# Twelve of 22 feed-forward groups in seven-product form, woven by written counts, and a planner that books durations as intervals with a lag

## Chip, cores and metric

The kernel runs on one core of a Trainium2 chip. The metric is the device time of one execution in microseconds; before the change it is 2728.07 us, the median of three runs (2727.68 to 2728.62).

## What is computed

A trunk of two decoder layers over 256 tokens of width 2048 in float32: layer 0 mixes tokens with a gated DeltaNet, layer 1 with HGRN2, and each is followed by a SwiGLU feed-forward of inner width 5632. The change touches the two feed-forwards and the order of everything.

```python
def swiglu(h, w_gate, w_up, w_down):
    return (jax.nn.silu(h @ w_gate) * (h @ w_up)) @ w_down

def reference(x, ...):
    h = x
    for layer in range(DEPTH):
        ...
        h = h + gdn_mixer(...)      # layer 0; hgrn2_mixer in layer 1
        h = h + swiglu(rmsnorm(h, ffn_norm[layer]), ffn_w_gate[layer], ffn_w_up[layer], ffn_w_down[layer])
    return rmsnorm(h, final_norm)
```

## The kernel before

**Products in three parts.** Weights arrive as tiles of 128 x 1024 float32 (512 KB, `raw`, loaded by SP). ScalarE (ACT) rounds such a tile to the short format fp32r (`wh`), VectorE (DVE) subtracts to get the rest (`wl`), and TensorE (PE) forms high x high, high x low and low x high for each product. The activations stand split in the same way (`xt_h`, `xt_l`). One such weight tile with its load, its split and its products is an `Item`; `stream` takes the items in one list, prepares three ahead (`AHEAD`), and `wh` and `wl` have four buffers each, `raw` four.

**The feed-forward.** `ffn` cuts the inner width into 22 groups of 256 gate and 256 up columns. A plain group (`gate_up`) is 8 items, each 12 products of 512 columns into a two-bank PSUM tile `main`, and at its end the gate and the product with it. A seven-product group (`mixed_group`) computes the 2 x 2 blocks (two halves of the tokens, gate and up against two halves of the inner sum) with seven block products in place of eight, by Strassen's scheme in Winograd's form: 4 rounds of 4 items with 1, 2, 2 and 2 block products, each block product 2 x 3 matrix products of 256 columns into four banks `aux`. For each round two weight tiles are loaded (`sraw`), and two more tiles of sums of weight blocks are made on DVE with four additions of 512 columns; all four come from one ring of four `sraw` buffers, so that the next load of a half waits until the last addition on the tile before has read it. At its end eight DVE operations join the seven products (`p1`, `p4`, `sg`, `h1`). Sums of the activations' blocks (`mixh`, `mixl`) are made once a layer by `mix_inputs`. The finished groups are turned in pairs through DRAM (`turned`, `blocks_home`) and split again (`hth`, `htl`), and `down` multiplies them in four parts with 24, 24, 24 and 16 items; a part's result is added to the running sum in DRAM (`x_home`) by an accumulating DMA of POOL, four of 512 KB a part.

**What sets the order.** `FF_PLAN` has a line for each of the four parts: what stands alone, then the seven-product groups, the plain items among which their items are woven, and two numbers for `among`: how many plain items stand ahead of the first and behind the last woven one. `among` spreads the items evenly, in pairs. Nine groups are in seven-product form (2, 6, 7, 9, 12, 13, 15, 18, 20). PE's main products run in this list's order.

All operations of the program are recorded first (`Recorder`), then `plan` simulates the engines with booked costs (`COST`, `HOP`, `LANDING` and so on) and issues everything in the order in which it started; the order on each engine, and each queue's, is fixed by that. `price` books an operation; `late` is the time by which it should be done. For a DVE or ACT operation the booked cost is the whole time from its start to its result, and the engine is booked for as long.

Of the kernel before, what the change touches and what calls it, by code (L numbers as in the profile page):

```python
# [23 lines left out]
N_FF = 22  # L24
FF_PARTS = (6, 6, 6, 4)
FF_PLAN = (
# [4 lines left out]
)  # L31
N_HGRN = 4
LEVELS = (64, 32, 16, 8, 4, 2, 1)
# [14 lines left out]
HOP = 0.2  # L48
PE_SLACK = 1.5
TURN = 0.06  # L50
FP32_PRODUCT = 0.224
NARROW = {32: 0.027, 64: 0.063}
COST = {
    ("vector", "tensor_tensor"): (0.14, 1.065e-3),
    ("vector", "scalar_tensor_tensor"): (0.205, 1.065e-3),
    ("vector", "tensor_scalar"): (0.16, 0.7e-3),
    ("vector", "tensor_single_scalar"): (0.16, 0.7e-3),
    ("vector", "tensor_copy"): (0.15, 0.6e-3),
    ("vector", "tensor_reduce"): (0.30, 1.0e-3),
    ("vector", "tensor_tensor_scan"): (0.15, 2.1e-3),  # L60
    ("vector", "copy_predicated"): (0.20, 1.3e-3),
    ("vector", "transpose"): (0.18, 1.0e-3),
    ("vector", "reciprocal"): (0.20, 1.0e-3),
    ("scalar", "activation"): (0.235, 0.82e-3),
    ("gpsimd", "tensor_tensor"): (0.10, 2.3e-3),
    ("gpsimd", "tensor_copy"): (0.20, 0.8e-3),
    ("gpsimd", "memset"): (0.10, 0.85e-3),
    ("gpsimd", "affine_select"): (0.1, 1.05e-3),
}
MARGIN = 1.02  # L70
POW = 1.3
LANDING_OF = {"wide": 7.0, "u": 7.0}
# [13 lines left out]


class Op:
    __slots__ = ("eng", "method", "args", "kw", "cost", "lag", "main", "pred", "succ", "n", "late", "call", "tiles", "heirs", "share")

    def __init__(self, eng, method, args, kw, cost=0.0, lag=0.0, main=False):
        self.eng, self.method, self.args, self.kw = eng, method, args, kw
        self.cost, self.lag, self.main = cost, lag, main
# [63 lines left out]
class Recorder:  # L157
# [110 lines left out]
    def price(self, op, out):  # L268
        n = int(np.prod(out.shape[1:]))
        if op.method == "dma_start":  # L270
            op.cost, op.lag = ISSUE[op.eng], LANDING[op.eng]
            op.share = n * out.shape[0] / (P * 1024)
            if (v := self.virtual(out)) and v.tag in LANDING_OF:
                op.lag = LANDING_OF[v.tag]
        elif op.eng == "tensor":
            if op.method == "matmul" and op.args[1].dtype == F32R:
                op.cost = 0.0133 + n / 2400.0
            elif op.method == "transpose":
                op.cost = 0.112
            else:  # L280
                m = op.args[1].shape[1]
                op.cost = NARROW[m] if m <= 64 else max(FP32_PRODUCT, n * 1.69e-3)
        else:
            fixed, each = COST[op.eng, op.method]
            if op.method == "tensor_reduce":
                n = int(np.prod(op.kw["in_"].shape[1:]))
            op.cost = (fixed + each * n) * MARGIN
            if op.kw.get("accum_out") is not None:
                op.cost += ACCUMULATE
            if op.eng == "gpsimd" and op.kw.get("op") == ALU.pow:  # L290
                op.cost = POW
# [24 lines left out]
    def plan(self):  # L316
# [6 lines left out]
        t = 0.0  # L323
# [4 lines left out]
        end = t  # L328
        for op in reversed(ops):
            late = min((s.late for s in op.succ + op.heirs if s.n > op.n), default=end)  # L330
            late -= op.cost + op.lag + HOP
# [55 lines left out]
        while len(order) < len(ops):  # L387
            e, at = min(
                ((e, s) for e in clock if (s := start_of(e)) is not None), key=lambda x: x[1]
            )  # L390
            while waiting[e] and waiting[e][0][0] <= at:
                _, n, op = heapq.heappop(waiting[e])
                heapq.heappush(ready[e], (op.late, n, op))
            op = heapq.heappop(ready[e])[2] if ready[e] else mains.pop()
            wait = place(op, at)
            if wait is not None:
                if isinstance(wait, tuple):
                    starved.setdefault(wait, []).append(op)
# [12 lines left out]
            self.at[op.n] = at  # L411
            order.append(op)
            done = at + op.cost
            clock[e] = at + max(0.45, LOAD_EVERY * op.share) if e == "sync" else done
            for v in op.tiles:
                v.left -= 1
                v.free = max(v.free, done + op.lag + HOP)
                if not v.left:
                    v.pool.slots[v.tag].append((v.free, v.slot))
                    for other in starved.pop((v.pool, v.tag), ()):  # L420
                        ready_at[other.n] = max(ready_at[other.n], at)
                        release(other)
            for s in op.succ:
                if e == "none" or s.eng == "none":
                    t = at
                elif e == "sync" and s.eng == e:
                    t = done
                elif s.eng == e and (e == "tensor" or not s.pred[op]):
                    t = done + op.lag
# [81 lines left out]
    return [c[:, at : at + 1024] for c in chunks for at in range(0, c.shape[1], 1024)]  # L511


def among(few, many, head, tail):

    out, done = [], 0
    for i, item in enumerate(many):
        out.append(item)
        upto = max(0, min(len(few), -(-len(few) * (i + 1 - head) // (len(many) - head - tail))))
        upto = upto // 2 * 2  # L520
        out += few[done:upto]
        done = upto
    return out


class Trunk:
# [359 lines left out]
    def ffn(self, j, after):  # L886
        nc, a = self.nc, self.a
        hts, h1s, quick, done = {}, {}, {}, set()
# [197 lines left out]
        items, waiting = [], None  # L1086
        for part, steps in enumerate(FF_PLAN):
            for step in steps.split(" | "):
                few, _, rest = step.partition(" : ")
                if not rest:  # L1090
                    items += gate_up(int(step))
                    continue
                beside, tail = rest.split(" : ")
# [6 lines left out]
                spare = (int(n) for n in tail.split())  # L1100
                items += among([i for g in few.split() for i in mixed_group(int(g))], many, *spare)
# [925 lines left out]
```

## Time and profile before

| | us |
|---|---|
| median of three runs | 2728.07 |
| the profiled execution | 2730.16 |
| its span, first to last instruction | 2728.5 |
| of it DeltaNet stage, first feed-forward, HGRN2 stage, second feed-forward | about 817, 695, 496, 720 |
| DVE busy in these four stretches | 624.85, 568.18, 365.67, 578.76 |
| ACT busy in them | 518.43, 389.21, 293.46, 394.90 |
| DMA: moved over the span | 599.64 MB, 220 GB/s in the mean |

A line of a group reads: source line, engine, operation, output<-inputs, shapes, count, then busy us and mean ns of one, then the engine's idle time before it with who ended it. All operations have one line number, that of `issue`, since they are recorded first, so groups are told apart by the names of their tiles. A row of waits reads: who waited <- for whom: total us, times, longest. A row of the timeline or of the chain starts with its time from the span's start and its length. A row of stretches has, after the stretch and its length, busy us and count for PE, PE's weight loads, DVE, ACT and POOL, then the clock granted to PE, the share of the DMA engines and GB/s. PE's rows overlap each other, so that the distance of starts, not the length of a row, is what a product costs.

### The profile page before, as it was taken

The numbers are of one execution on the slowest core, as the hardware profiler recorded it, in microseconds if no ns is written. First come the engines' busy times: TensorE is split into PE (matmuls) and PEld (weight loads), VectorE is DVE, ScalarE is ACT, GpSimd is POOL, SyncE is SP. The second block draws the span as 40 slices with busy tenths as digits, with TensorE's granted clock in tenths as the row PEclk, the third lists the DMA queues.
The fourth block names the chain that finished last, engine by engine and source line by source line (L and its number), as shares of the span: only waits on it lengthen the run. The fifth ranks groups of instructions, "written<-read, shape, count | busy, mean of one in ns | idle before, by whom it ended". The sixth has DMA issues, their size and how long they took to land.

```text
span 2728.5 us, 44570 instructions
## 1 busy us (share of the span) xinstructions
PE 2707.1 (99%) x16966; PEld 2352.0 (86%) x16966; DVE 2137.5 (78%) x3221; ACT 1596.0 (58%) x2246; POOL 326.6 (12%) x466
## 2 busy tenths in 40 slices
PE   9999999999999999999999999999999999999998
PEld 9888888888888888888888989988888888888886
DVE  7787888777758788888788688788578788888786
ACT  6646667566565555565555656556465555555554
POOL 2213222232110000000100100000110000000010
PEclk9999999999999999999999999999999999999999
DMA  8686578687686677777776755555776777677775
GB/s 277 202 282 213 188 224 242 212 262 209 214 241 211 219 232 217 238 219 223 243 229 213 238 168 185 166 167 178 198 262 206 229 217 237 223 225 226 232 230 194
DMA packets 173959, 599.64 MB, mean 220 GB/s; under 512 B 21674, under 2 KB 22842, under 8 KB 173616
## 3 DMA queue, kind: packets, MB, share of 16 engines
q1 hardware_dynamic: 138912, 503.15, 56.2%
q0 software_dynamic: 34544, 92.79, 13.6%
q8 instruction: 133, 2.18, 0.3%
q10 hardware_dynamic: 288, 0.85, 0.1%
q14 instruction: 82, 0.67, 0.1%
HBM read 550.52 MB, written 48.28 MB: 219 GB/s over the span
## 4 chain that ended last, share of the span: by engine, by line
PE 94%; DVE 2%; DMA 2%; ACT 1%; issue 1%; SPq 0%; POOLq 0%; POOL 0%; ACTq 0%; DVEq 0%
PE main L498 77%; PE aux L498 18%; DMA sraw<-in_ffn_gu 1%; DVE wl L498 1%; DVE turned L498 0%; DMA raw<-in_ffn_gu 0%; ACT wh L498 0%; DVE sraw L498 0%; DMA first<-in_x 0%; ACT dec L498 0%; DVE htl L498 0%; DVE h L498 0%; DVE utmp L498 0%; DVE pre L498 0%; SPq L498 0%
## 5 line engine op out<-in xcount | busy, mean ns | idle before, releaser
L498 ACT ACTIVATE wh<-raw 128x1024 fp32r<-128x1024 f32 x801 | 846.6, 1060 | 846.9 <-PE main L498 732.2
L498 DVE TENSOR_TENSOR wl<-raw,wh 128x1024 fp32r<-128x1024 f32 x801 | 980.9, 1227 | 404.8 <-ACT wh L498 389.2
L498 PE MATMUL main<-wh,xt_h 128*128 128x512 f32 x1600 | 626.1, 391 | 0.8 <-ACT wh L498 0.8
L498 PE MATMUL main<-wl,xt_h 128*128 128x512 f32 x1600 | 625.6, 391 | 1.3 <-DVE wl L498 1.3
L498 PE MATMUL main<-wh,xt_l 128*128 128x512 f32 x1600 | 625.2, 391 | 0.0
L498 ACT ACTIVATE wh<-sraw 128x1024 fp32r<-128x1024 f32 (+1 forms) x288 | 272.1, 950 | 170.2 <-PE main L498 100.5
L498 DVE TENSOR_TENSOR wl<-sraw,wh 128x1024 fp32r<-128x1024 f32 (+1 forms) x288 | 307.5, 1087 | 71.1 <-ACT wh L498 70.6
L498 PEld LDWEIGHTS main<-wh,xt_l 128*128 128x128 f32 x1600 | 300.4, 188 | 62.4
L498 PEld LDWEIGHTS main<-wh,xt_h 128*128 128x128 f32 x1600 | 300.3, 188 | 61.4 <-ACT wh L498 1.2
L498 PEld LDWEIGHTS main<-wl,xt_h 128*128 128x128 f32 x1600 | 300.4, 188 | 60.6 <-DVE wl L498 1.6
L498 PE MATMUL main<-xt_h,wh 128*128 128x256 f32 (+1 forms) x1040 | 288.7, 278 | 0.7 <-ACT wh L498 0.7
L498 PE MATMUL main<-xt_h,wl 128*128 128x256 f32 (+1 forms) x1040 | 288.3, 277 | 0.9 <-DVE wl L498 0.9
L498 PE MATMUL main<-xt_l,wh 128*128 128x256 f32 (+1 forms) x1040 | 288.1, 277 | 0.3 <-DVE xt_l L498 0.3
L498 PE MATMUL main<-wh,hth 128*128 128x512 f32 x688 | 268.8, 391 | 0.9 <-ACT hth L498 0.9
L498 PE MATMUL main<-wl,hth 128*128 128x512 f32 x688 | 269.0, 391 | 0.1
L498 PE MATMUL main<-wh,htl 128*128 128x512 f32 x688 | 268.0, 390 | 0.2
L498 PE MATMUL aux<-wl,mixh 128*128 128x256 f32 x864 | 239.6, 277 | 3.2 <-DVE wl L498 3.2
L498 PE MATMUL aux<-wh,mixh 128*128 128x256 f32 x864 | 239.2, 277 | 0.1
L498 PE MATMUL aux<-wh,mixl 128*128 128x256 f32 x864 | 239.1, 277 | 0.0
L498 PEld LDWEIGHTS main<-xt_h,wh 128*128 128x128 f32 (+1 forms) x1040 | 194.4, 187 | 1.3 <-ACT wh L498 0.9
L498 PEld LDWEIGHTS main<-xt_h,wl 128*128 128x128 f32 (+1 forms) x1040 | 194.4, 187 | 1.2 <-DVE wl L498 1.1
L498 PEld LDWEIGHTS main<-xt_l,wh 128*128 128x128 f32 (+1 forms) x1040 | 194.4, 187 | 1.0 <-DVE xt_l L498 0.5
(241 smaller groups left out, 3948.0 us busy)
## 6 DMA issues: line engine op xcount, KB each, us to landing
raw<-in_ffn_gu SPq DMA_DIRECT2D x208, 512.0 KB, 4.7
raw<-in_ffn_d SPq DMA_DIRECT2D x176, 512.0 KB, 5.0
sraw<-in_ffn_gu SPq DMA_DIRECT2D x144, 512.0 KB, 5.9
raw<-in_hgrn_in SPq DMA_DIRECT2D x128, 512.0 KB, 4.1
raw<-in_gdn_kq SPq DMA_DIRECT2D x64, 512.0 KB, 5.5
raw<-in_gdn_v SPq DMA_DIRECT2D x64, 512.0 KB, 4.6
raw<-in_gdn_z SPq DMA_DIRECT2D x64, 512.0 KB, 4.9
raw<-in_gdn_out SPq DMA_DIRECT2D x64, 512.0 KB, 5.3
```

Source lines behind the costliest of these rows:

```text
L498: getattr(getattr(tc.nc, op.eng), op.method)(*args, **kw)
```

## The change

```diff
@@ -24,10 +24,10 @@
 FF_PLAN = (
-    "0 | 2 : 1 3 4 5 : 6 2",
-    "6 7 9 : 8 down 10 11 : 4 4",
...
+    "0 | 2 4 : 1 3 5 : 010000413403001303131130",
+    "6 7 9 11 : 8 down 10 : 0041413002012050340022061033120300062102",
+    "12 13 15 17 : 14 down 16 : 0111053032003031304050231322022202002501",
...
@@ -49,24 +49,26 @@
+PRODUCT = 0.1136
...
 COST = {
-    ("vector", "tensor_tensor"): (0.14, 1.065e-3),
...
+    ("vector", "tensor_tensor"): (0.065, 1.055e-3),
...
-    ("scalar", "activation"): (0.235, 0.82e-3),
+    ("scalar", "activation"): (0.14, 0.82e-3),
...
+TAIL = {"vector": 0.08, "scalar": 0.095}
@@ -274,7 +276,7 @@
             if op.method == "matmul" and op.args[1].dtype == F32R:
-                op.cost = 0.0133 + n / 2400.0
+                op.cost = PRODUCT * n / 256
@@ -285,6 +287,7 @@
             op.cost = (fixed + each * n) * MARGIN
+            op.tail = TAIL.get(op.eng, 0.0)
@@ -428,9 +431,9 @@
                 elif s.eng == e and (e == "tensor" or not s.pred[op]):
                     t = done + op.lag
                 elif s.eng == "tensor" and not s.main:
-                    t = done + op.lag + HOP + PE_SLACK
+                    t = done + op.lag + op.tail + HOP + PE_SLACK
                 else:
-                    t = done + op.lag + HOP
+                    t = done + op.lag + op.tail + HOP
@@ -511,15 +514,11 @@
-def among(few, many, head, tail):
+def woven(few, many, pattern):
-    out, done = [], 0
-    for i, item in enumerate(many):
-        out.append(item)
-        upto = max(0, min(len(few), -(-len(few) * (i + 1 - head) // (len(many) - head - tail))))
-        upto = upto // 2 * 2
-        out += few[done:upto]
-        done = upto
+    out, few = [], iter(few)
+    for item, n in zip(many, pattern):
+        out += [item] + [next(few) for _ in range(int(n))]
     return out
```

Groups 4, 11 and 17 change from the plain to the seven-product form in each layer, so that twelve of 22 have it. The even spreading gives way to a written digit for each plain item: so many seven-product items follow it. The fourth line keeps its groups and gets digits too. In the planner the fixed part of every DVE and ACT cost is cut by about what its rows overlap the next one, and that much is added as a lag (`tail`) ahead of whoever needs the result; a fp32r product of 256 columns is booked at 0.1136 in place of 0.12. `tail` is taken off in `late` and added where a tile comes free, too.

By count of instructions PE loses 576 products of 512 columns and gains 1008 of 256; DVE gets 96 additions of 512 columns more, 24 more short and 72 more long splits of `sraw` tiles, 48 fewer of `raw` tiles, and the six groups' ends; ACT the same splits; SP issues 48 `sraw` loads in place of 48 `raw` ones. Everything else keeps its number.

Two places in the order matter below. The first is DVE, in the second stretch of the first feed-forward, from the addition that frees a ring buffer to the first additions on the tile loaded into it. Before, from the group's joint (freed by the first row, read anew in the last; `x2` is two in a row):

```order
L498 TENSOR_TENSOR sraw_1775_11244<-sraw_1775_11244,sraw_1757_11095 128x512
L498 TENSOR_TENSOR sraw_1793_11291<-sraw_1781_11212 128x512
L498 TENSOR_TENSOR h1_1645_10698<-h1_1645_10698,sg_1747_11205 128x256
L498 TENSOR_TENSOR h1_1645_10698<-h1_1645_10698,sg_1748_11281 128x256
L498 TENSOR_TENSOR wl_1777_11308<-sraw_1775_11244,wh_1776_11294 128x1024
L498 TENSOR_TENSOR wl_1780_11315<-raw_1778_11164,wh_1779_11305 128x1024
L498 TENSOR_TENSOR wl_1783_11331<-sraw_1781_11212,wh_1782_11320 128x2x256
L498 STREAM_TRANSPOSE turned_1749_11342<-h1_1645_10698 128x256 x2
L498 TENSOR_TENSOR sraw_1793_11291<-sraw_1784_11296,sraw_1781_11212 128x512
```

With the change, at one of its joints (the last row reads the new tile `sraw_1891`):

```order
L501 TENSOR_TENSOR sraw_1885_11805<-sraw_1885_11805,sraw_1879_11709 128x512
L501 STREAM_TRANSPOSE turned_1838_11827<-h1_1631_10594 128x256 x2
L501 TENSOR_TENSOR wl_1884_11836<-sraw_1882_11704,wh_1883_11820 128x1024
L501 STREAM_TRANSPOSE turned_1838_11827<-h1_1631_10594 128x256
L501 TENSOR_TENSOR sraw_1894_11848<-sraw_1888_11784 128x512
L501 STREAM_TRANSPOSE turned_1838_11827<-h1_1631_10594 128x256
L501 TENSOR_TENSOR wl_1887_11856<-sraw_1885_11805,wh_1886_11842 128x1024
L501 TENSOR_TENSOR sraw_1894_11848<-sraw_1891_11830,sraw_1888_11784 128x512
```

Between the two ends stood two long splits, a short one, one addition and four smaller operations; now there stand two long splits, one addition and four transposes.

The second place is ACT in the DeltaNet stage, the third block of 24 decay rows (`dec` from `g_row`) of a head group among the weight splits `wh`. Before:

```order
L498 ACTIVATE wh_4431<-raw_4285 128x1024
L498 ACTIVATE junk_66,so_4462<-aux_4452 128x128 x4
L498 ACTIVATE dec_4484<-g_row_3569,shift_360 128x64 x24
L498 ACT_TABLE_LOAD
L498 ACTIVATE dec_4484<-dec_4484 128x1536
```

With the change:

```order
L501 ACTIVATE wh_4181<-raw_4076 128x1024
L501 ACTIVATE junk_66,so_4206<-aux_4198 128x128 x4
L501 ACTIVATE dec_4226<-g_row_3296,shift_346 128x64 x5
L501 ACTIVATE wh_4238<-raw_4107 128x1024
L501 ACTIVATE dec_4226<-g_row_3296,shift_346 128x64 x9
L501 ACTIVATE wh_4269<-raw_4140 128x1024
L501 ACTIVATE dec_4226<-g_row_3296,shift_346 128x64 x9
L501 ACTIVATE wh_4302<-raw_4171 128x1024
L501 ACTIVATE dec_4226<-g_row_3296,shift_346 128x64
L501 ACT_TABLE_LOAD
```

Three weight splits, which stood behind the block, now stand in it; the two blocks of 24 ahead of this one stay whole, and elsewhere runs of six rows between splits have become runs of nine.

More of the change, by code (lines that the diff above doesn't have):

```diff
@@ L51 @@
 FP32_PRODUCT = 0.224
+PRODUCT = 0.1136
 NARROW = {32: 0.027, 64: 0.063}
 COST = {
-    ("vector", "tensor_tensor"): (0.14, 1.065e-3),
[L55 to L61, printed above, removed]
+    ("vector", "tensor_tensor"): (0.065, 1.055e-3),
+    ("vector", "scalar_tensor_tensor"): (0.127, 1.06e-3),
+    ("vector", "tensor_scalar"): (0.08, 0.7e-3),
+    ("vector", "tensor_single_scalar"): (0.08, 0.7e-3),
+    ("vector", "tensor_copy"): (0.07, 0.6e-3),
+    ("vector", "tensor_reduce"): (0.22, 1.0e-3),
+    ("vector", "tensor_tensor_scan"): (0.07, 2.1e-3),
+    ("vector", "copy_predicated"): (0.16, 1.3e-3),
     ("vector", "transpose"): (0.18, 1.0e-3),
-    ("vector", "reciprocal"): (0.20, 1.0e-3),
-    ("scalar", "activation"): (0.235, 0.82e-3),
+    ("vector", "reciprocal"): (0.12, 1.0e-3),
+    ("scalar", "activation"): (0.14, 0.82e-3),
     ("gpsimd", "tensor_tensor"): (0.10, 2.3e-3),
@@ L88 @@
 class Op:
-    __slots__ = ("eng", "method", "args", "kw", "cost", "lag", "main", "pred", "succ", "n", "late", "call", "tiles", "heirs", "share")
+    __slots__ = ("eng", "method", "args", "kw", "cost", "lag", "main", "pred", "succ", "n", "late", "tail", "call", "tiles", "heirs", "share")
     def __init__(self, eng, method, args, kw, cost=0.0, lag=0.0, main=False):
         self.eng, self.method, self.args, self.kw = eng, method, args, kw
-        self.cost, self.lag, self.main = cost, lag, main
+        self.cost, self.lag, self.main, self.tail = cost, lag, main, 0.0
         self.pred, self.succ = {}, []
@@ L330, in plan @@
             late = min((s.late for s in op.succ + op.heirs if s.n > op.n), default=end)
-            late -= op.cost + op.lag + HOP
+            late -= op.cost + op.lag + op.tail + HOP
             op.late = min(op.late, late) if op.main else late
@@ L416, in plan @@
                 v.left -= 1
-                v.free = max(v.free, done + op.lag + HOP)
+                v.free = max(v.free, done + op.lag + op.tail + HOP)
                 if not v.left:
@@ L1092, in ffn @@
                     continue
-                beside, tail = rest.split(" : ")
+                beside, pattern = rest.split(" : ")
                 many = []
@@ L1099, in ffn @@
                         many += gate_up(int(g))
-                spare = (int(n) for n in tail.split())
-                items += among([i for g in few.split() for i in mixed_group(int(g))], many, *spare)
+                few = [i for g in few.split() for i in mixed_group(int(g))]
+                assert len(pattern) == len(many) and sum(map(int, pattern)) == len(few)
+                items += woven(few, many, pattern)
             assert waiting is None
```

3 rows, old and new, of the table FF_PLAN are left out of this document.

## The prediction

> **What bounds the kernel now.** I read the page first, then who waits on PE, then the chain of waits for PE's pace, then the stretches of the feed-forward stages.
>
> ```profile
> span 2728.5 us, 44570 instructions
> PE 2707.1 (99%) x16966; PEld 2352.0 (86%) x16966; DVE 2137.5 (78%) x3221; ACT 1596.0 (58%) x2246; POOL 326.6 (12%) x466
> ...
> PE aux L498 <- DVE wl L498: 3.2, 4, 0.9
> PE main L498 <- DVE wl L498: 2.2, 2, 1.3
> PE main L498 <- ACT wh L498: 1.5, 2, 0.8
> ```
>
> PE is busy 99% and waits for others only some 7 us in these three rows, with no wait over 1.3 us. So the time is the number of PE's products times their pace, and a change gains by taking products away and loses by making PE wait. The pace:
>
> ```profile
> 946.50 21.79 PE main L498 x96
> ...
> 901.22 0.28 PE L498 MATMUL aux<-wh,mixh 128*128 128x256 f32 x1
> ...
> 903.84 0.28 PE L498 MATMUL aux<-wh,mixl 128*128 128x256 f32 x1
> ```
>
> The first row is 96 products of 512 columns in a row: 21.79/96 = 0.2270 us each. The other two are the first and the last of 24 products of 256 columns: (903.84 - 901.22)/23 = 0.1139 us each, half of it, though a row lasts 0.28 us, since products overlap.
>
> The engine to watch behind PE is DVE. In the second stretch of a feed-forward stage, where three seven-product groups are woven into plain ones:
>
> ```profile
> 970.00:1130.00 160.00, 159.00 (x928) 140.06 (x927) 132.42 (x157) 91.92 (x102) 10.16 (x14) 1.00 0.77 229
> ...
> 1084.83 8.44 DMA sraw<-in_ffn_gu
> 1275.33 8.02 DMA sraw<-in_ffn_gu
> 2275.55 7.86 DMA sraw<-in_ffn_gu
> 2465.45 7.92 DMA sraw<-in_ffn_gu
> ```
>
> DVE (third number with a count) is busy 132.42 of 160 us, ACT 91.92, PE 159.00, at a granted clock of 1.00. The four later rows are the only ring loads on the chain that ended last: one in the second and one in the third stretch of each layer. Each is followed by one of the four waits "PE aux <- DVE wl" above.
>
> **The change part by part.** *Products.* Six groups (three a layer) change form. Each loses 96 products of 512 columns, 96 x 0.2270 = 21.79 us, and gains 4 x 2 x 7 x 3 = 168 of 256 columns, 168 x 0.1139 = 19.14 us. The gain is 2.65 us a group, **-15.9 us** in all. All of it lies on the path, since PE is the bound.
>
> The Trainium skill ("TensorE: Matmul & The Clock Gate", Back-to-back issue gap) has a warm product cost its columns over 2.4 GHz and a fixed 2.5 ns, which speaks against many short products. By that the two forms would be 20.7 and 18.3 us, and the gain an estimated 14.2 us, 1.7 less than the sum takes. The rows above show no such fixed part here (0.2270 against 2 x 0.1139).
>
> *DVE.* What such a group asks of it, beside a plain one:
>
> ```profile
> L498 DVE TENSOR_TENSOR wl<-raw,wh 128x1024 fp32r<-128x1024 f32 x801 | 980.9, 1227 | 404.8 <-ACT wh L498 389.2 <-PE aux L498 3.6 <-PE main L498 2.0
> L498 DVE TENSOR_TENSOR sraw<-sraw,sraw 128x512 f32<-128x512 f32 x216 | 146.9, 686 | 18.6 <-DMA sraw<-in_ffn_gu 17.8
> L498 DVE SCALAR_TENSOR_TENSOR p<-aux,rstd,p 128x256 f32<-128x256 f32 x36 | 17.3, 481 | 0.6
> L498 DVE TENSOR_TENSOR p<-aux,p 128x256 f32<-128x256 f32 x36 | 15.2, 422 | 1.9 <-PE aux L498 0.9
> L498 DVE TENSOR_TENSOR h<-h,sg 128x256 f32<-128x256 f32 x36 | 14.5, 418 | 0.0
> L498 DVE TENSOR_TENSOR h<-aux,sg 128x512 f32<-128x512 f32 x18 | 12.3, 681 | 0.0
> ...
> 1084.11 0.68 DVE L498 TENSOR_TENSOR sraw<-sraw,sraw 128x512 f32<-128x512 f32 x1
> 1084.71 0.69 DVE L498 TENSOR_TENSOR sraw<-sraw 128x512 f32<-128x512 f32 x1
> 1085.32 0.75 DVE L498 TENSOR_TENSOR h<-h,sg 128x256 f32<-128x256 f32 x2
> 1086.01 1.23 DVE L498 TENSOR_TENSOR wl<-sraw,wh 128x1024 fp32r<-128x1024 f32 x1
> 1087.15 1.22 DVE L498 TENSOR_TENSOR wl<-raw,wh 128x1024 fp32r<-128x1024 f32 x1
> 1088.95 0.69 DVE L498 TENSOR_TENSOR wl<-sraw,wh 128x512 fp32r<-128x512 f32 x1 [0.59 <-ACT wh L498]
> 1089.56 0.76 DVE L498 STREAM_TRANSPOSE turned<-h 128x256 f32<-128x256 f32 x2
> 1093.29 1.29 DVE L498 TENSOR_TENSOR sraw<-sraw,sraw 128x512 f32<-128x512 f32 x2 [2.97 <-DMA sraw<-in_ffn_gu]
> ```
>
> Starts stand closer than durations: an add of 512 starts 0.60 us before the next (1084.11, 1084.71), a split of 1024 1.14 us (1086.01, 1087.15); some 0.08 us overlap. By these starts a seven-product group has 16 adds (9.6), 4 short splits (2.4), 12 long ones (13.7), eight operations at its end (by the four rows about 3.7 less 8 x 0.08: 3.1) and its share of turning, about 1.2: 30.0 us. A plain one has 8 long splits (9.1), two products with the gate (0.8) and the turning: 11.1. So DVE has 18.9 us more to do a group. The second stretch of a layer then has 4 x 30.0 + 2 x 11.1 + 24 x 1.14 = 169.6 us of DVE work beside 4 x 19.14 + 2 x 21.79 + 288 x 0.2270 = 185.5 us of PE: 91%, where it was 80% (151 of 188). The third is alike, the first has about 90%, the last is unchanged in its sum. DVE does not become the bound, but its free time in a full stretch falls from 37 to 16 us, so a delay is made good more slowly. At the joint of two groups PE's first product into a bank also stands right behind the read of that bank (groups 12 and 13). I take one wait a layer at the longest that PE shows above, 1.3 us, less a little: **+2**. Bounds: 0, and one such wait at each of the eight joints a layer, +21.
>
> *The ring of loads.* This is the term that decides. A seven-product group reads 8 loads of 512 KB through a ring of four tiles, and the next load of a half waits until the last add on the old one is done. What DVE has in its order between that add and the first add on the new tile covers the load. Counted in the built order with the starts above, the cover was never under 4.8 us: 4 of 144 loads had 4.8, 22 had 5.1. Now 20 of 192 loads have 4.8 or less (3.5 to 4.7), and 16 more up to 5.15. The four at 4.8 before are the four chain rows. The DVE rows just shown are the first of them: the add at 1084.11 frees the tile, DVE runs out of work at 1090.32, the load lands at 1084.83 + 8.44 = 1093.27, and PE feels it:
>
> ```profile
> 1083.96 1.19 POOL L498 DMA_DIRECT2D x_home<-x  x1 [23.76 <-ACT sg L498]
> ...
> 1094.11 0.28 PE L498 MATMUL aux<-wh,xt_l 128*128 128x256 f32 x1
> 1094.49 0.38 PE L498 MATMUL aux<-wh,mixh 128*128 128x256 f32 x1
> 1095.78 0.39 PE L498 MATMUL aux<-wl,mixh 128*128 128x256 f32 x1 [0.91 <-DVE wl L498]
> ...
> sraw<-in_ffn_gu SPq DMA_DIRECT2D x144, 512.0 KB, 5.9
> x_home<-x POOLq DMA_DIRECT2D x52, 512.0 KB, 8.6
> ```
>
> Two starts are late by 0.26 and 1.17 us beside the pace, 1.4; with the smaller three I price a late load at 1.1 us, so 4.4 us are paid now. The load is slow (8.44 against a median of 5.9) because POOL had just issued an accumulation into x_home, which takes 8.6. How many of the 20 meet one? Four transfers fall in a stretch of 185 us; each disturbs loads issued over about 8.6 + 5.9 us, 58 of 185, so 6 of 20 if they fell at random, and all 20 if they are as aligned as the four were. I take 9, nearer to chance, since the new digits spread the loads: 9 x 1.1 - 4.4 = **+5.5**. Bounds: -4.4 (none) and (20 + 16/2) x 1.1 - 4.4 = +26.4.
>
> *The planner's costs.* All stages are put in a new order. In the feed-forward and HGRN2 stages little can move, PE waiting there only for the rows named. In the DeltaNet stage the waits "PE main" above (2.2 and 1.5) follow blocks of 24 decay rows on ACT that no weight split interrupts:
>
> ```profile
> 294.04 5.86 ACT dec L498 x24
> ...
> L498 ACT ACTIVATE wh<-raw 128x1024 fp32r<-128x1024 f32 x801 | 846.6, 1060 | 846.9 <-PE main L498 732.2
> ```
>
> Three such blocks stood there; two remain, and the third is cut into runs of 5, 9, 9 and 1 with a split between. That saves about half of those waits. Against it, runs of 6 became runs of 9 elsewhere: 5.86/24 = 0.244 us a row, so 9 rows and a split of 1.06 take 3.3 us where a weight item lasts 12 x 0.2270 = 2.72, half a microsecond late a run, over some ten such runs; the three items split ahead should hide it. I take **-1**. Bounds: -3.7 (all these waits gone) and +5.
>
> Loads of plain weights, stores and the kernel's end keep their number. The sum: -15.9 + 2 + 5.5 - 1 = **-9.4**. The profiled execution took 2730.16 us around its span of 2728.5, the median of three runs is 2728.07; applied to the median the forecast is **2719 us**.
>
> **Rivals.** *(a) The ring is no tighter in practice: 2711.* Only as many loads are late as before, so -15.9 - 1. For it: half of the loads land within the median of 5.9 us, and DVE's own idle time adds to the cover. Against: DVE has less idle time now.
>
> *(b) The ring decides, slower: 2740.* All 20 loads up to 4.8 us and half of the next 16 come late: +26.4 - 15.9 + 2 = +12.5. It overtakes the gain from (15.9 + 4.4)/1.1 = about 18 late loads on. For it: before, four of four at the edge were late. Against: these four were one place repeated four times.
>
> *(c) DVE is the bound: 2740.* If an operation kept DVE for its whole duration (0.08 us more than the starts say), a seven-product group would take 33.6 us, a plain one 12.2, and the second stretch 4 x 33.6 + 2 x 12.2 + 24 x 1.23 = 188 us against 185.5 of PE: +2.5 in each of four such stretches, and with no free time left each of the 20 loads would cost its 1.1 (+17.6 over now): +10 + 17.6 - 15.9 = +12. Against it stand the starts 0.60 us apart. The Trainium skill ("VectorE: DVE Perf Modes", Terms, DRAIN) says that the next operation cannot issue until the pipe is empty, which read as the whole duration would make this the outcome; the trace does not bear that reading out (0.60 between starts, 0.68 long).
>
> *(d) The new order costs in DeltaNet: 2726.* The runs of nine come late after all: +5 and some of the saved wait back. For it: three items of lead hid runs of six, and no run of nine but one stands in the trace. Against: that one brought no wait on PE.
>
> **How the numbers follow.** Forecast 0.48, (a) 0.22, (b) 0.13, (c) 0.04, (d) 0.13. The likeliest one's own range is 2714 to 2725. To hold 8 in 10 the range takes in (a) and (d) and stops short of (b): 2709 to 2734. A change under 0.2% (5.5 us, 2722.6 to 2733.5) cannot be told from none. Faster: 0.40 of the forecast, all of (a), 0.04 of (d): 0.66. Slower: 0.09 of (b) and (c): 0.13. Same: 0.21.
>
> **What would show it.** In the new profile, 3456 "aux<-...mixh/mixl" products at starts of 0.114 us confirm the first term. DVE should read 90 to 96% in the second stretch (83% in the row above). "PE aux <- DVE wl" should be about ten waits and some 10 us; four waits speak for (a), twenty or more for (b), and "DVE wl <- ACT wh" near nothing for (c). "PE main <- ACT wh" or "<- DVE wl" over 5 us before 817 us speaks for (d). The forecast is wrong if PE's waits together exceed some 20 us, or if the time falls under 2709.

## The result, and the profile after

The changed kernel takes **2735.22 us** (median; 2728.51 to 2741.69) against 2727.68 us before (2726.27 to 2730.79): ratio 1.0029, 95% interval 1.0023 to 1.0035. It is 0.29% slower, where 2719 us was forecast. The profiled execution took 2737.94 us.

The page of the changed kernel: its first rows, the chain that ended last by engine, one row of its groups and one of its transfers:

```profile
span 2736.2 us, 45703 instructions
PE 2704.2 (99%) x17398; PEld 2367.1 (87%) x17398; DVE 2235.8 (82%) x3401; ACT 1631.4 (60%) x2300; POOL 326.1 (12%) x466
...
PE 85%; DVE 6%; DMA 6%; ACT 1%; issue 1%; POOL 0%; SPq 0%; POOLq 0%; DVEq 0%; ACTq 0%
...
L501 DVE TENSOR_TENSOR sraw<-sraw,sraw 128x512 f32<-128x512 f32 x288 | 194.2, 687 | 37.1 <-DMA sraw<-in_ffn_gu 36.5
...
sraw<-in_ffn_gu SPq DMA_DIRECT2D x192, 512.0 KB, 5.1
```

In the kernel before the chain's row was:

```profile
PE 94%; DVE 2%; DMA 2%; ACT 1%; issue 1%; SPq 0%; POOLq 0%; POOL 0%; ACTq 0%; DVEq 0%
```

PE is still busy 99%, and with fewer columns to multiply. But the chain now lies 6% on DMA and 6% on DVE, where it was 2% and 2%, and the additions of the ring waited 36.5 us for their loads instead of 17.8. The loads' median is lower than before (5.1 against 5.9), so it is not the typical load that is late. Who waits, in the changed kernel (us in total, times, longest):

```profile
PE main L501 <- DVE wl L501: 6.5, 8, 0.9
PE aux L501 <- DVE wl L501: 4.7, 7, 1.6
PE aux L501 <- DMA first<-in_x: 2.2, 1, 2.2
PE aux L501 <- ACT wh L501: 1.6, 1, 1.6
...
DVE sraw L501 <- DMA sraw<-in_ffn_gu: 48.6, 36, 3.5
...
ACT wh L501 <- DMA sraw<-in_ffn_gu: 55.6, 31, 5.2
```

In the kernel before, DVE's row was 11 waits and ACT's 4:

```profile
DVE sraw L498 <- DMA sraw<-in_ffn_gu: 17.8, 11, 3.0
...
ACT wh L498 <- DMA sraw<-in_ffn_gu: 16.3, 4, 4.5
```

PE's own rows look harmless: they list a delay only where it is long. The better measure is PE's starts. For each product of 512 or 256 columns I took the time to the next start and subtracted 0.2272 or 0.1136 us, which is what the new planner books for it. Summed over the two feed-forward stages (812 to 1515 us, and from 2010 us on), PE started late by 12.2 us before and by 31.6 us in the changed kernel. The experiments below use this sum as "PE late".

One late load of the changed kernel, as the timeline shows it (start, us, engine, line, operation, tiles; in brackets the idle time before and who ended it):

```profile
2170.08 0.56 POOL L501 DMA_DIRECT2D blocks_home<-turned  x1 [35.38 <-DVE turned L501]
2170.80 0.70 DVE L501 TENSOR_TENSOR sraw<-sraw,sraw 128x512 f32<-128x512 f32 x1
2171.34 0.69 SPq L501 DMA_DIRECT2D sraw<-in_ffn_gu  x1
...
2173.84 0.56 POOL L501 DMA_DIRECT2D turned<-blocks_home  x1 [3.20 <-ACT wh L501]
2175.04 1.64 POOL L501 DMA_DIRECT2D turned<-blocks_home  x3 [0.64 <-issue]
...
2179.83 0.69 DVE L501 TENSOR_TENSOR sraw<-sraw 128x512 f32<-128x512 f32 x1 [3.48 <-DMA sraw<-in_ffn_gu]
2179.84 0.28 PE L501 MATMUL aux<-wh,mixh 128*128 128x256 f32 x1
...
2181.71 0.39 PE L501 MATMUL aux<-wl,mixh 128*128 128x256 f32 x1 [1.60 <-DVE wl L501]
```

The addition at 2170.80 frees the tile and SP issues the next load at 2171.34. POOL's transfers for turning h run beside it, and it lands only about 8.4 us later. DVE has nothing else to do for 3.48 us, then catches up, and PE's product at 2181.71 starts 1.87 us after the one before instead of 0.11. No accumulation into x_home is near. The prediction had named only those as what slows a load.

Counted over the 192 ring loads of this trace: 84 had no transfer of POOL on either DRAM tile beside them (median 4.6 us, 5 of them over 6.5), 51 ran beside one on x_home (median 6.4, 25 over 6.5) and 57 beside the turning alone (median 6.3, 25 over 6.5). Of the 36 additions that waited for a load, 14 (17.2 us of the 48.6) waited for one that had run beside a transfer on x_home, 21 (30.4 us) for one beside the turning alone, and one (1.0 us) for one beside neither. In the kernel before it was the other way round: 8 of the 11 waits (14.9 of 17.8 us) were for loads beside a transfer on x_home.

### The profile page after: what moved, and what is told of

Read it like the earlier page. It is cut to its first block, busy times and chain, and to the rows that moved or that the text cites. A ratio compares the mean times of both kernels' runs of the same rounds, so it can differ in the third digit from the quotient of the medians.

```text
span 2736.2 us, 45703 instructions
## 1 busy us (share of the span) xinstructions
PE 2704.2 (99%) x17398; PEld 2367.1 (87%) x17398; DVE 2235.8 (82%) x3401; ACT 1631.4 (60%) x2300; POOL 326.1 (12%) x466
## 4 chain that ended last, share of the span: by engine, by line
PE 85%; DVE 6%; DMA 6%; ACT 1%; issue 1%; POOL 0%; SPq 0%; POOLq 0%; DVEq 0%; ACTq 0%
PE main L501 67%; PE aux L501 18%; DMA sraw<-in_ffn_gu 4%; DVE wl L501 3%; DVE sraw L501 1%; ACT wh L501 1%; DVE turned L501 1%; ACT dec L501 0%; DMA raw<-in_gdn_kq 0%; DMA raw<-in_ffn_gu 0%; DMA turned<-blocks_home 0%; DVE h L501 0%; DMA blocks_home<-turned 0%; DVE p L501 0%; DVE htl L501 0%
## 5 line engine op out<-in xcount | busy, mean ns | idle before, releaser
L501 PE MATMUL main<-wh,xt_h 128*128 128x512 f32 x1408 | 551.4, 392 | 1.2 <-ACT wh L501 1.2
L501 PE MATMUL main<-wh,xt_l 128*128 128x512 f32 x1408 | 551.2, 391 | 0.0
L501 ACT ACTIVATE wh<-sraw 128x1024 fp32r<-128x1024 f32 (+1 forms) x384 | 362.8, 952 | 310.5 <-PE main L501 176.4
L501 DVE TENSOR_TENSOR wl<-sraw,wh 128x1024 fp32r<-128x1024 f32 (+1 forms) x384 | 412.7, 1087 | 45.5 <-ACT wh L501 44.1
L501 PE MATMUL aux<-wl,mixh 128*128 128x256 f32 x1152 | 321.4, 279 | 5.0 <-DVE wl L501 4.7
L501 PE MATMUL aux<-wh,mixh 128*128 128x256 f32 x1152 | 319.7, 278 | 1.6 <-ACT wh L501 1.6
L501 PE MATMUL aux<-wh,mixl 128*128 128x256 f32 x1152 | 319.7, 278 | 0.0
L501 PEld LDWEIGHTS aux<-wl,mixh 128*128 128x128 f32 x1152 | 217.0, 188 | 12.0 <-DVE wl L501 7.8
L501 DVE TENSOR_TENSOR sraw<-sraw,sraw 128x512 f32<-128x512 f32 x288 | 194.2, 687 | 37.1 <-DMA sraw<-in_ffn_gu 36.5
L501 PEld LDWEIGHTS aux<-wh,mixh 128*128 128x128 f32 x1152 | 217.3, 189 | 6.0 <-ACT wh L501 1.8
```

Of the source, the lines that this page charges most:

```text
L501: getattr(getattr(tc.nc, op.eng), op.method)(*args, **kw)
```

## The experiments

All runs in one table. "PE late" is the sum defined above; the last column is the row "DVE sraw <- DMA sraw" (us and times). Ratios are against runs of the kernel before on the same chip. Its medians there were 2727.68 to 2729.12 us, so a difference between the medians of two rows is uncertain by up to some 1.4 us.

| run | median us | ratio to before (95%) | PE late, us | DVE waits for ring loads |
|---|---|---|---|---|
| before | 2727.68 | 1 | 12.2 | 17.8, 11 |
| changed | 2735.22 | 1.0029 (1.0023 to 1.0035) | 31.6 | 48.6, 36 |
| old_costs | 2790.6 | 1.0229 (1.0215 to 1.0243) | 83.1 | 55.7, 38 |
| new_costs | 2727.28 | 0.9994 (0.9986 to 1.0003) | 7.3 | 4.5, 7 |
| no_ring_loads | 2713.53 | 0.9948 (0.9936 to 0.9961) | 11.5 | none |
| ring5 | 2723.18 | 0.9977 (0.9968 to 0.9986) | 17.4 | 18.7, 17 |
| no_x_home | 2725.62 | 0.9990 (0.9981 to 0.9999) | 23.4 | 36.7, 25 |
| no_turn | 2730.47 | 1.0006 (0.9997 to 1.0015) | 25.8 | 21.9, 16 |
| no_side | 2722.79 | 0.9979 (0.9969 to 0.9988) | 18.7 | 12.7, 10 |
| before_no_ring | 2724.95 | 0.9985 (0.9976 to 0.9994) | 7.0 | none |
| inplace | 2739.2 | 1.0040 (1.0027 to 1.0052) | 35.2 | none |
| before_inplace | 2733.77 | 1.0017 (1.0008 to 1.0026) | 15.0 | none |
| s0_ring5 | 2729.57 | 1.0004 (0.9995 to 1.0013) | 27.6 | none |
| even | 2745.06 | 1.0063 (1.0050 to 1.0076) | 47.1 | 31.2, 28 |
| land8_ring5 | 2715.25 | 0.9952 (0.9938 to 0.9965) | 11.4 | 1.3, 1 |
| land8_ring4 | 2843.08 | 1.0426 (1.0412 to 1.0440) | 146.5 | 15.0, 10 |
| land8_six | 2727.34 | 0.9994 (0.9986 to 1.0003) | 7.4 | 0.3, 1 |

### Which part of the change costs

**old_costs.** The changed kernel with the planner's table of before.

```diff
-    ("vector", "tensor_tensor"): (0.065, 1.055e-3),
+    ("vector", "tensor_tensor"): (0.14, 1.065e-3),
...
-TAIL = {"vector": 0.08, "scalar": 0.095}
+TAIL = {}
...
-                op.cost = PRODUCT * n / 256
+                op.cost = 0.0133 + n / 2400.0
```

> The changed kernel with the planner's costs of before (twelve groups, the new digits). Three theories for the 17 us between the forecast of the sum of products (2712) and the 2735 measured. T1, late ring loads: the cover of the ring is about as thin here (22 of 192 loads at 4.8 us or less, 20 in the changed kernel), so 2731 to 2737. T2, VectorE is nearly full and makes delays good too slowly: its work is the same, so 2733 to 2737. T3, the new order (its waits and the clock drops behind them): all of it goes, 2720 to 2727.

(2735 less 2712 is 23 us; the 17 there is a slip.) It came out at 2790.6, far outside all three. The written digits only work together with the new costs. With the old ones the order makes PE wait for h itself as well:

```profile
PE aux L501 <- DVE wl L501: 17.9, 21, 2.0
PE main L501 <- DVE htl L501: 9.8, 6, 2.4
PE main L501 <- ACT hth L501: 9.7, 5, 2.4
```

In the changed kernel's list the second of these rows is missing and the third is one wait of 0.3 us. So T3 in the form "the new costs are what is paid for" falls; the costs are needed.

**new_costs.** The kernel before with the new table alone (the reverse of that diff, applied to the kernel before).

> The kernel before (six groups, even weaving) with the new planner's costs alone. T1: 6 of 144 loads at 4.8 us or less against 4, so 2727 to 2731. T2: 2726 to 2730. T3, the new order: 2734 to 2740, with the clock at half at some 220 and 490 us as in the changed kernel.

2727.28 us, no change that can be told, within the ranges of T1 and T2. T3 falls here too. Under the unchanged total two things moved: DVE's waits for ring loads fell from 17.8 to 4.5 us and PE late from 12.2 to 7.3; what took that gain away again is in the table of stages further down.

**no_ring_loads.** The two halves of a weight piece (the tiles that one round of a seven-product group loads) come from two tiles loaded once a layer.

```diff
-                    item(kk, halves[0], keep(0), [(1, lambda k: k * 512)], lambda x: quarters(x)[:, 0]),
+                    item(kk, None, keep(0), [(1, lambda k: k * 512)], lambda x: quarters(x)[:, 0], kept(0, halves[0])),
...
-                return self.tile(self.pool, [P, 1024], "sraw", bufs=4, ordered=True)
+                return self.tile(self.pool, [P, 1024], "sraw", bufs=2, ordered=True)
```

> The changed kernel with the ring's loads left out: each layer loads two halves of a weight group once and all seven-product groups read these two tiles, so the groups' values are not the reference's; additions, splits and products stay in number. T1: no wait for a ring load is left, so 2719 to 2724. T2: VectorE has the same work, so 2731 to 2736. T3: 2731 to 2736.

2713.53 us, 21.7 less than the changed kernel, below even T1's range. So more than the whole loss hangs on the ring's loads. By itself this run can't tell their lateness from their traffic, which is gone with them; ring5 and land8_ring5 below keep every load. The run also decides T2 as it was put. In the second stretch (us, then busy time and count of PE, PEld, DVE, ACT, POOL, granted clock, DMA share, GB/s), first the changed kernel:

```profile
970.00:1130.00 160.00, 158.77 (x977) 141.50 (x976) 145.27 (x185) 94.43 (x105) 13.21 (x19) 1.00 0.77 232
```

and without the ring's loads:

```profile
970.00:1130.00 160.00, 160.00 (x1001) 143.93 (x1000) 148.68 (x186) 97.63 (x108) 13.21 (x19) 1.00 0.51 143
```

DVE is even fuller here, 148.68 of 160 us or 93%, and PE is never idle. A DVE at 93% does not by itself hold PE up. Whether a DVE with more free time would pass on less of a late load was not tried.

**ring5.** Five ring tiles; room comes from a scratch tile in bfloat16 and from the last rows' tile lying in h1.

```diff
-                return self.tile(self.pool, [P, 1024], "sraw", bufs=4, ordered=True)
+                return self.tile(self.pool, [P, 1024], "sraw", bufs=5, ordered=True)
...
-        self.junk = t([P, 512], "junk")
+        self.junk = t([P, 512], "junk", mybir.dt.bfloat16)
```

> The changed kernel with a ring of five tiles instead of four (room for it from a 2-byte scratch output of squares and from the last rows' tile lying in h1): 8 of 192 loads have a cover of 4.8 us or less instead of 20, the median cover is 8.1 us instead of 6.4. T1: 2720 to 2727. T2: 2732 to 2736. T3: 2732 to 2736.

2723.18 us, T1's case: 12 of the 21.7 us are back with every load, addition and product still there, and the traffic no smaller.

### What makes the loads late

**no_x_home** leaves out the accumulations of the first three parts; **no_turn** leaves out the turning's way through DRAM; **no_side** leaves out both.

```diff
             self.nc.scalar.activation(more, ps, AF.Copy)
-            self.nc.gpsimd.dma_start(self.x_cols(self.x_home, cg), more, accum_op=ALU.add)
```

```diff
-        self.nc.gpsimd.dma_start(home, blocks)
...
-        return out
+        return blocks
```

> The changed kernel with the 24 accumulations of the first three parts into x_home left out (their sums are missing in the output). After the first four runs the ring's loads carry the loss; open is what makes them late. A, the accumulations alone, as the prediction had it: most of the 21.7 us that leaving out the ring's loads gave, so 2715 to 2720. B, the transfers that turn h through DRAM as well: VectorE stood 17.2 us before late ring loads that met an accumulation and 30.4 us before such that met a turning, so a third of 21.7, 2726 to 2730. C, the thin cover with no collision: 2733 to 2736.

> The changed kernel with the way through DRAM left out of the turning (five transfers of POOL a pair of groups; the pairs' values stay unturned, so the output is not the reference's). A: 2733 to 2736. B: two thirds of 21.7 gone, 2719 to 2724. C: 2733 to 2736.

> The changed kernel without the accumulations of the first three parts into x_home and without the way of the turning through DRAM (both left out, so the output is not the reference's). One by one they gave 9.6 and 4.7 us of the 21.7 that the ring's loads cost. If collisions are all of it: 2713 to 2717. If the two only add up and the rest is the thin cover beside the other weight loads: 2719 to 2723.

The accumulations are worth 9.6 us (2735.2 less 2725.6), the turning 4.7, both 12.4, as in the second case of no_side. Neither A nor B was right in size: the accumulations weigh more than B's share and the turning less, and A's "most of 21.7" is not reached either. With both gone, 9 us of the 21.7 remain, so loads are late also without a collision with POOL's transfers. The trace of no_side shows beside what: 141 of its ring loads shared over 3 us with other weight loads and nothing of POOL's (median 4.9 us, longest 7.8), 45 shared less (median 3.9, longest 4.9). That the other weight loads are the reason was not tried by a run.

**before_no_ring.** The kernel before, its ring's loads left out in the same way as in no_ring_loads.

> The kernel before with its ring's loads left out in the same way (two halves a layer are loaded once; the groups' values are not the reference's). The prediction priced what late ring loads cost there at 4.4 us: 2723 to 2725. If its eleven waits of VectorE for a ring load cost 1.1 us each: 2714 to 2718. If nothing of them reaches TensorE: 2727 to 2729.

2724.95 us: late ring loads cost the kernel before 4.1 us (against 2729.06 in the same set of runs), and 4.4 was the prediction's price.

### More cover: three ways

**inplace** and **before_inplace** write the four sums over the loaded tiles, so that a piece takes two ring tiles instead of four. **s0_ring5** does so for the first two sums only, with five tiles.

```diff
-                        raws[2] = t[:, 0]
-                        add(t[:, 0], b11, b12)
-                        add(t[:, 1], b22, b12)
+                        add(b11, b11, b12)
+                        add(b12, b22, b12)
...
-                        add(t[:, 0], b22, raws[2])
-                        add(t[:, 1], t[:, 0], b21)
+                        add(b22, b22, b11)
+                        add(b21, b22, b21)
```

> The changed kernel with the four sums of a weight piece written over the two loaded tiles instead of into two more tiles of the ring, so that four tiles hold two pieces instead of one; all transfers, additions, splits and products stay. Counted in the built order the cover of a ring load rises from a median of 6.4 to 13.6 us, none under 6. If the wait for the ring loads is what costs: 2712 to 2717, as without these loads. If it was their traffic that slowed other things: 2723 to 2735. If additions in place wait for ScalarE's split of the same tile: 2718 to 2725 with 'DVE sraw <- ACT wh' in the waits.

> The kernel before with the same sums in place. The prediction priced its late ring loads at 4.4 us (four of them): 2722 to 2725. If only few of VectorE's 17.8 us of waits for them reach TensorE: 2726 to 2728. If eleven late loads cost 1.1 us each: 2714 to 2718.

> The changed kernel with five ring tiles and only the first pair of sums of a weight piece written over its loaded tile, so that a piece takes three tiles instead of four; counted in the built order the cover is never under 6 us (median 14.9). If late loads are the whole loss and the first sums can wait for the short split of 512 columns: 2713 to 2718. If sums in place cost as much as in the run with all four in place: 2728 to 2740.

inplace and before_inplace missed all their cases, with 2739.2 and 2733.8 us; s0_ring5, with 2729.6, is in its second. Almost no load is late any more. In the run inplace, and then in the changed kernel, ACT waits for DVE's sums:

```profile
ACT wh L501 <- DVE sraw L501: 84.4, 63, 3.4
...
PE aux L501 <- DVE wl L501: 12.4, 12, 2.0
```

```profile
ACT wh L501 <- DVE sraw L501: 25.2, 23, 3.1
```

A sum in place must wait until both splits of the loaded tile have read it, and the next split must wait for the sum. The late loads were exchanged for a longer chain of dependence between ACT and DVE; in s0_ring5 the row reads 96.1 us. These runs therefore say nothing on the price of the loads.

**even.** Twelve groups with the kernel before's spreading by pairs.

```diff
-    "0 | 2 4 : 1 3 5 : 010000413403001303131130",
+    "0 | 2 4 : 1 3 5 : 4 2",
```

> The changed kernel with its twelve groups spread evenly in pairs, as the kernel before spreads its six, instead of by the written digits; 16 of 192 loads have a cover of 4.8 us or less and 52 of 5.15 or less, against 20 and 36. If the cover at the edge decides: 2732 to 2742. If the digits bring the late loads by their bursts of four or more items: 2720 to 2728. If VectorE needs the digits to keep up: over 2745.

2745.06 us, 3 us beyond the first case and just inside the third (over 2745). The digits are worth 10 us over even pairs. The ring does not explain it: DVE waits less for ring loads here than in the changed kernel (31.2 us against 48.6), yet PE late is 47.1 us against 31.6, and PE waits for the splits:

```profile
PE aux L501 <- DVE wl L501: 20.5, 24, 1.6
```

In the changed kernel that row is 4.7 us in 7 waits. So the digits may bring late loads, and still pay by keeping the splits in time, which is the third case; no run tells this from other reasons.

### What the planner believes of a load

The planner takes 4.8 us for a load to land. With that figure it needs no more than 4.8 us of cover. **land8_ring5** and **land8_ring4** are ring5 and the changed kernel with 8.0 us; **land8_six** is new_costs with 8.0 us.

```diff
-LANDING_OF = {"wide": 7.0, "u": 7.0}
+LANDING_OF = {"wide": 7.0, "u": 7.0, "sraw": 8.0}
```

> The changed kernel with five ring tiles, and the planner told that a ring load lands after 8.0 us instead of 4.8; no sums in place. Counted in the built order 2 of 192 loads have a cover under 6 us (14 under 5.5 and 28 under 6 with five tiles alone, 52 and 74 in the changed kernel), with a median of 9.8. If the planned cover is what makes loads late: 2713 to 2718. If the later order takes VectorE's place from the plain splits: 2723 to 2732.

> The changed kernel with four ring tiles and the planner's landing time of a ring load at 8.0 us alone. 16 of 192 loads keep a cover of 4.8 us or less (20 before), 32 are under 5.5 (52 before). By the number of thin covers: 2728 to 2733. If the planner's figure alone were the fault: 2715 to 2724.

> The kernel before (six groups, even weaving, four ring tiles) with the new planner's costs and the landing time of 8.0 us: no cover under 5.0 us. Leaving out its ring's loads gave 4.1 us: if the cover is the cause, 2723 to 2727; if the loads' waits there are of another kind, 2727 to 2730.

land8_ring5 takes **2715.25 us**, 0.48% faster than the kernel before and 0.73% faster than the changed kernel. This is its first case. It is the fastest kernel that computes the reference. The collisions are still there (53 of its 192 ring loads run beside a transfer on x_home and 58 beside the turning, 51 and 57 in the changed kernel), and its loads are no faster. PE's and DVE's waits in it:

```profile
PE main L501 <- DVE wl L501: 1.9, 2, 1.0
PE aux L501 <- DVE p L501: 1.6, 2, 0.8
...
DVE sraw L501 <- DMA sraw<-in_ffn_gu: 1.3, 1, 1.3
```

```profile
sraw<-in_ffn_gu SPq DMA_DIRECT2D x192, 512.0 KB, 5.8
```

PE late is 11.4 us, as without the ring's loads (11.5). So cover is enough, and collisions decide only where it is short. land8_ring4 took 2843 us. The rows show that DVE's waits for ring loads did fall (15.0 us), but PE now waits for the splits:

```profile
PE aux L501 <- DVE wl L501: 48.6, 51, 2.5
...
PE aux L501 <- ACT wh L501: 28.5, 22, 3.3
```

My reading is that the planner, which must wait 8 us for each load and has four tiles, places a piece's sums so late that the piece is late by plan; the chip then follows that order however fast the load was. That reading was not tested by itself. The expectation had counted covers alone and missed it by 110 us. land8_six (2727.34 us) cannot be told from the kernel before or from new_costs: it fell in the second of its two cases, and DVE's waits for the ring were already down to 4.5 us with the new costs alone.

## Why the prediction was wrong, point by point

**Products, -15.9 us: right.** A row of twelve in the changed kernel shows the pace:

```profile
2174.34 0.28 PE L501 MATMUL aux<-wh,mixh 128*128 128x256 f32 x1
...
2175.60 0.28 PE L501 MATMUL aux<-wh,mixl 128*128 128x256 f32 x1
```

(2175.60 - 2174.34)/11 = 0.1145 us. There are 3 x 1152 such products. With the ring's loads out of both kernels the change is a gain of 11.4 us (2724.95 to 2713.53), or 10 by the two ratios. The stages by themselves, counted in the traces, tell more:

| stage, us | before | before_no_ring | new_costs | changed | no_ring_loads | land8_ring5 |
|---|---|---|---|---|---|---|
| DeltaNet | 824.67 | 826.39 | 826.69 | 828.05 | 824.39 | 826.88 |
| first feed-forward | 704.69 | 702.01 | 702.01 | 703.90 | 696.08 | 696.07 |
| HGRN2 | 486.03 | 486.03 | 487.49 | 487.49 | 487.49 | 487.49 |
| second feed-forward | 702.65 | 700.13 | 700.40 | 706.32 | 694.05 | 694.14 |

(One profiled execution each; the end of the kernel, 10 to 11 us, is left out. A mixer's stage is counted to the start of PE's last product on an `ot` tile, a feed-forward to that of its last product on an `ht` tile.) Without the ring's loads the two feed-forwards become 12.0 us shorter while PE late rises from 7.0 to 11.5, so the products gave some 16.5 us.

The estimate that the prediction draws from the Trainium skill ("TensorE: Matmul & The Clock Gate", Back-to-back issue gap) is further off: an estimated gain of 14.2 us, or 14.3 when its two terms are not rounded.

**DVE and the joints, +2: right in kind.** DVE is busy 91% in the second stretch, as worked out. At the joint of groups 12 and 13 PE starts 0.95 us late in each layer, 1.9 in all. The other 2.6 of the 4.5 us are delays under 0.3 us, most of them under 0.02 us a start, which the prediction had not priced.

**The ring, +5.5: the step that failed.** The mechanism was the one named as deciding. Its size was not: late loads cost 21.7 us in the changed kernel (no_ring_loads) against 4.1 before, so +17.6; by the feed-forward stages of the table it is 20.1 against 5.2, so +14.9. The sentence at fault is "How many of the 20 meet one? ... I take 9". It took only loads with at most 4.8 us of cover as at risk, and only accumulations into x_home as what delays a load. In the trace 36 additions waited for a load, 21 of them for one beside the turning alone. Counted in the trace, with 0.08 us taken off each duration, 17 of the 36 had at most 4.8 us of cover and 15 more under 6; their loads took 6.0 to 9.9 us to land. For 14 of the 36 it was DVE's split of the old tile that freed it, and not the last addition on it.

For the kernel before, count and price held: behind the four loads that the prediction took PE started late by 1.44, 1.01, 0.85 and 0.91 us, 4.2 in all, and behind DVE's other seven waits no start was late by over 0.25 us. In the changed kernel 18 starts are late by more than that which have no counterpart without the ring's loads, 14.5 us in all; the rest is in smaller delays. For each of DVE's 36 waits that is less than the price of 1.1 us: 21.7/36 is 0.6 us. So the count was too low by much more than the price was too high.

**The planner's costs, -1: not told apart from nothing in the total, and wrong in its parts.** new_costs can't be told from the kernel before (0.9986 to 1.0003). In DeltaNet, where the prediction put its gain, PE, DVE and ACT work in one and the same order in all 13 runs with the new costs; the stage took 823.5 to 828.1 us there, 825.5 in the mean, and 825.5 in the mean of the four with the old costs (824.7 to 826.4). In HGRN2, where "little can move", the stage is 1.5 us longer in every run with the new costs: PE's small products `aux<-qp,kp` and `aux<-q_last,k` take 18.0 and 5.0 us of its time instead of 16.7 and 4.1. In the feed-forwards the new costs by themselves gained 4.9 us in the kernel before, nearly the 5.2 that leaving out its ring's loads gave.

Added up in medians, the ring's +17.6 less the 11.4 us gained without it (the planner's costs are contained in that) make +6.2; measured were +7.5. The kernel before itself gave medians of 2727.7 to 2729.1 us from one set of runs to the next, so these 1.3 us are no more than its scatter. In the two profiled executions the difference is 7.8 us: 2.9 in the feed-forwards (-12.0 and +14.9), 1.5 in HGRN2 and 3.4 in DeltaNet, where other executions of the same order were as short as 823.5 us.

**The rivals.** (b), the ring decides, 2740 us, is what happened, at two thirds of its price (17.6 of 26.4). (a) falls with no_ring_loads, which shows the ring's price. (c) falls with the same run, and "DVE wl <- ACT wh" stands at 341.6 us, so DVE has slack. (d) falls with new_costs and with the means of DeltaNet just given; "PE main <- ACT wh" and "<- DVE wl" before 812 us come to 3.1 us.

**What was to show it.** "About ten waits and some 10 us" of "PE aux <- DVE wl" would have misled: 7 waits and 4.7 us stand there, between (a) and the forecast, and the time was nearer (b)'s. Part of the difference stands in another row: "PE main <- DVE wl" has six waits of 4.6 us in all at plain items of the feed-forwards, and none there without the ring's loads. The rest is delays of PE too short for this view.

## What to carry to other kernels

When a change raises the load of a helper engine, count what that engine's work was covering: here it was DVE's own queue between freeing a buffer and needing it again. Judge the cover against the slow landings beside other transfers (6 to 10 us for those that came late here), not against the median (5), and give the planner that figure together with the buffers to hold it, because either alone was worth less or did harm. Judge the bound engine by its starts, not only by its listed waits.

## What the runs showed of the hardware that was not expected

The granted clock fell to half for 3.41 us behind stretches of that length in which PE was not idle throughout. In the changed kernel this happened at 219.7, 489.3 and 2520.2 us; the kernel before had a drop only at its very end, as every run has. The stretch before the last of the three and the drop itself:

```profile
2516.80:2520.20 3.40, 0.85 (x5) 0.46 (x4) 2.67 (x4) 2.59 (x3) 0.00 (x0) 1.00 0.28 99
2520.20:2523.60 3.40, 3.40 (x17) 3.40 (x18) 3.40 (x4) 2.74 (x4) 0.00 (x0) 0.51 0.65 225
```

PE was busy for 0.85 of the 3.40 us before. Around 219.7 us it had been busy for longer:

```profile
216.30:219.70 3.40, 1.79 (x6) 1.10 (x7) 2.76 (x4) 3.40 (x4) 1.67 (x3) 0.99 0.37 127
219.70:223.10 3.40, 3.40 (x23) 2.03 (x22) 2.48 (x7) 3.31 (x9) 0.23 (x1) 0.50 0.73 247
```

The Trainium skill ("TensorE: Matmul & The Clock Gate", Part 1: The HAM clock gate, What's actually happening) has the clock fall after an idle window of about 3.4 us; the length of the drop agrees, but here a window with 0.85 or 1.79 us of work in it was followed by a drop.

Such a stretch does not always bring one. All 13 runs with the new costs have the same waits before the same products near 219 us; a drop followed in six of them and none in seven. In no_ring_loads, with the same 1.79 us of work:

```profile
216.07:219.47 3.40, 1.79 (x6) 1.10 (x7) 2.75 (x4) 3.40 (x4) 1.67 (x3) 1.00 0.29 111
219.47:222.87 3.40, 3.40 (x30) 2.43 (x29) 3.14 (x10) 3.31 (x9) 0.64 (x2) 1.00 0.82 276
```

What decides between the two was not found. Half the clock for 3.41 us is worth an estimated 1.7 us of products, so a wait of some 2 us can cost nearly as much again where a drop follows. The DeltaNet stage of the 13 runs fits that: it took 823.5 to 824.6 us in the five without a drop in it, 824.6 to 826.8 in the four with one, and 826.0 to 828.1 in the four with two. The profiled executions of old_costs and land8_ring4 had seven and more drops ahead of the last, those of the other runs none to two, some at other places, so they are not tied to one order. Whether they are behind the wider spread of the changed kernel (13 us from lowest to highest, 4.5 before) was not tried.
